# First products of eight channel blocks ahead of the norm: a hybrid attention block on one Trainium2 core

## The chip, the core and the metric

One core of a Trainium2 chip runs the whole kernel: TensorE (PE; its weight load is the row PEld), VectorE (DVE), ScalarE (ACT), GpSimd (POOL) and SyncE (SP), which issues most of the transfers. SBUF has 128 partitions, and TensorE adds up in PSUM. The metric is the device time of one execution in microseconds (us). The three runs shown of the kernel before have a median of 1760.35 us (1759.39 to 1760.63).

## The reference, cut to what matters

A layer works on 256 latent tokens `x` and 256 context tokens `ctx`, each of 2048 channels. The change touches its first step only, the modulated RMS norm and the input projection:

```python
sh1, sc1, g1, sh2, sc2, g2 = jnp.split(jax.nn.silu(c) @ w_ada[l] + b_ada[l], 6, axis=-1)
csh1, csc1, ... = jnp.split(jax.nn.silu(c_ctx) @ w_ada[l] + b_ada[l], 6, axis=-1)
... = split_columns(modulate(rmsnorm(x, norm_mix[l]), sh1, sc1) @ w_in[l])
... = split_columns(modulate(rmsnorm(ctx, norm_mix[l]), csh1, csc1) @ w_in[l])
# rmsnorm(x, w) = x * rsqrt(mean(x * x) + eps) * w;  modulate(x, shift, scale) = x * (1 + scale) + shift
```

So the input of the projection is h = x · a · r + shift, where a = w(1 + scale) and the shift go by channel and the norm r by token. Everything else (latent attention, a gated DeltaNet in both directions, the merge, a gated MLP) comes behind it and is the same in both kernels.

## The kernel before, in words

Channels lie on partitions: 16 blocks of 128 channels (`KD`), and 2 × 256 tokens as columns (latent and context, the two streams s). All products are done with a high and a low half: a number is rounded to the type fp32r (its high half), and the rest is its low half; a product is high·high + high·low + low·high. `load_w` and `split` make the halves of a weight, ScalarE the high (line 123), VectorE the low (line 124), in six buffers each.

The first stage runs in an order written out by hand. `pe`, `oact`, `odve` and `osync` are engines whose instructions keep the order of the program (`Ordered`); instructions of the plain `act`, `dve`, `sync` are placed by the compiler's scheduler between them. It goes as follows:

- The scale and the shift by channel come from products of `silu(c)` with 4096 columns of `w_ada`, in two ways. `mod_mm` (16 products of 256 columns, 32 output rows each, tile `amp`) and `mod_cols` (turn the row into columns, tiles `aas` for a and `shs` for the shift) give two blocks at once from a quad of 512 KB weight tiles. `scale_dot` gives the scale of one block on VectorE, by two dots of 2048 elements (tile `junk`) with rows that `spread` copied to all partitions (tile `scb`). The blocks in `SCP`, counted in pairs, get their scale in the first way, the others by dots; every shift comes in the first way.
- Squares of x and ctx (tile `sq`), their sum over channels (`square_sum`, tile `pss`), the norm r on GpSimd and its broadcast to a tile `bc` come ahead of the first product.
- Then block by block (loop over k at line 481): `first_hi` casts the weight of 864 columns (96 + 6 × 128) to its high half `gh`; `h_prep` takes x · a · r, adds the shift and makes both halves of h (two fused multiplies, two activations, two fused adds, and the weight's low half `gl`); `first_mm` does 7 column tiles × 2 streams × 3 products, added up over all 16 blocks in 7 PSUM banks (`fp`). Between the tiles lie the modulation products of later blocks, behind them the dots.
- The seven sums are copied to `krd` and `dkx`, and the general projections (`proj`, tile `mmp`) go on with all 16 blocks of h, which stays in SBUF (`H`).

SP issues the loads in written order; a load waits for its buffer, and so do the loads behind it. There are 8 tiles of 512 KB (`raw`: quads of `mod_mm`, later the weights of `proj` and of the modulation's rest), 4 of 1 MB (`wt`) and 3 of a first weight's 432 KB (`gr`).

Of the kernel before, what the change touches and what calls it, by code (L numbers as in the profile page):

```python
# [45 lines left out]
NW = 4  # L46
SCP = (0, 2, 4, 6)
# [8 lines left out]
def hybrid_block(ctx: ExitStack, tc: tile.TileContext, io, dbg=None):  # L56
# [285 lines left out]
    def mod_cols(p, scale, amp, row):  # L342
# [3 lines left out]
        for j in range(2):  # L346
            k = slice(2 * p + j, 2 * p + j + 1)
            out, mul, add = (aas, nmix[:, k], b1[:, k]) if scale else (shs, 1.0, bada[:, k])
            oact.activation(out[:, 2 * p + j], amp[:, T + 2 * j : T + 2 * j + 2], AF.Identity, bias=add, scale=mul)

    def load_scale(k):
        w = pa2.tile([P, D], F32, tag="wt", name="wt", bufs=NW)
        osync.dma_start(w, io["wadas"][k])
        return w

    scm = {}
# [10 lines left out]
    def load_first(k):
        gr = pa2.tile([P, G3], F32, tag="gr", name="gr", bufs=3)
        osync.dma_start(gr, io["wfirst"][k])
        return gr  # L370

    def first_hi(k):

        g = [pa2.tile([P, G3], F32R, tag=n, name=n) for n in ("gh", "gl")]
        oact.copy(g[0], grs[k])
        return g

    def h_prep(k, gh, gl):

        late = k and k % 2 == 0 and k // 2 in SCP  # L380
        if late:
            odve.tensor_tensor(out=gl, in0=grs.pop(k), in1=gh, op=ALU.subtract)
        for s, xs in enumerate((xl, xc)):
            odve.scalar_tensor_tensor(out=xs[:, k], in0=xs[:, k], scalar=aas[:, k, s : s + 1], in1=(bc if k else bcp)[:, s], op0=ALU.mult, op1=ALU.mult)
        if not late:
            odve.tensor_tensor(out=gl, in0=grs.pop(k), in1=gh, op=ALU.subtract)
        for s, xs in enumerate((xl, xc)):
            oact.activation(H[s][:, k, 0], xs[:, k], AF.Identity, bias=shs[:, k, s : s + 1], scale=1.0)
        for s, xs in enumerate((xl, xc)):
# [1312 lines left out]
```

## Time and profile before

| | us |
|---|---|
| median of the runs shown | 1760.35 |
| the profiled execution | 1757.95 |
| its span, first to last instruction | 1756.1 |
| TensorE busy in the span | 1733.0 |
| VectorE busy | 1333.7 |
| ScalarE busy | 943.1 |
| first product of the first stage starts at | 29.1 |
| first product of the projections starts at | 141.06 |

The profile is of one execution. Its rows give the start or the number of instructions, busy time, engine, line and operation, and in brackets the idle time of the engine just before with what ended it. Nearly all instructions of the ordered engines carry line 70, that of the helper which records them, so they are told apart by their tiles. The engines wait for each other through semaphores, and idle time of an engine costs only where TensorE, busy 99% of the span, ends up waiting for it.

### The profile page before, as it was taken

The numbers are of one execution on the slowest core, as the hardware profiler recorded it, in microseconds if no ns is written. First come the engines' busy times: TensorE is split into PE (matmuls) and PEld (weight loads), VectorE is DVE, ScalarE is ACT, GpSimd is POOL, SyncE is SP. The second block draws the span as 40 slices with busy tenths as digits, with TensorE's granted clock in tenths as the row PEclk, the third lists the DMA queues.
The fourth block names the chain that finished last, engine by engine and source line by source line (L and its number), as shares of the span: only waits on it lengthen the run. The fifth ranks groups of instructions, "written<-read, shape, count | busy, mean of one in ns | idle before, by whom it ended". The sixth has DMA issues, their size and how long they took to land.

```text
span 1756.1 us, 34353 instructions
## 1 busy us (share of the span) xinstructions
PE 1733.0 (99%) x13093; PEld 1507.0 (86%) x13093; DVE 1333.7 (76%) x2608; ACT 943.1 (54%) x1953; POOL 48.5 (3%) x49
## 2 busy tenths in 40 slices
PE   8999999999999999999999999999999999999999
PEld 6787888888888888888888888888888888888888
DVE  4688887679888778686789788887787888655554
ACT  4235545454566756665665555555555555544443
POOL 0000001000000000000000000000000000000000
PEclk9999999999999999999999999999999999999999
DMA  9993788683788777897958757777667777566662
GB/s 383 392 374 130 204 257 239 204 275 108 242 248 244 237 240 245 289 331 262 340 167 264 266 176 254 237 231 234 188 217 223 228 227 226 177 203 202 193 198 89
DMA packets 188566, 414.56 MB, mean 236 GB/s; under 512 B 56752, under 2 KB 95024, under 8 KB 186096
## 3 DMA queue, kind: packets, MB, share of 16 engines
q1 hardware_dynamic: 162800, 397.39, 69.9%
q10 hardware_dynamic: 25600, 14.96, 2.8%
q8 instruction: 103, 1.69, 0.4%
q14 instruction: 63, 0.52, 0.1%
HBM read 385.69 MB, written 26.48 MB: 235 GB/s over the span
## 4 chain that ended last, share of the span: by engine, by line
PE 89%; DMA 5%; DVE 3%; issue 1%; ACT 1%; SPq 0%; POOL 0%; POOLq 0%; ACTq 0%; DVEq 0%
PE fps L70 27%; PE dps L70 14%; PE mmp L70 13%; PE gtp L70 10%; PE brp L70 5%; PE ops L70 4%; PE fp L70 4%; DMA raw<-in_wadab 1%; PE vps L70 1%; PE amp L70 1%; PE kps L70 1%; DVE wlo L124 1%; PE tp L70 1%; DMA rawa<-in_wada 1%; PE kp L70 1%
## 5 line engine op out<-in xcount | busy, mean ns | idle before, releaser
L124 DVE TENSOR_TENSOR wlo<-raw,whi 128x512 fp32r<-128x512 f32 (+1 forms) x940 | 635.4, 685 | 211.0 <-ACT whi L123 200.0
L123 ACT CAST whi<-raw 128x512 fp32r<-128x512 f32 (+1 forms) x940 | 574.4, 619 | 377.7 <-PE dps L70 113.7
L70 PE MATMUL fps<-H,whi 128*128 128x512 f32 x1376 | 472.6, 392 | 1.4 <-DVE H L1537 1.4
L70 PE MATMUL fps<-H,wlo 128*128 128x256 f32 x1376 | 371.5, 280 | 0.0
L70 PEld LDWEIGHTS fps<-H,whi 128*128 128x128 f32 x1376 | 252.5, 188 | 52.6 <-ACT whi L123 1.7
L70 PEld LDWEIGHTS fps<-H,wlo 128*128 128x128 f32 x1376 | 258.5, 188 | 7.6 <-DVE wlo L124 0.7
L70 PE MATMUL gtp<-h,whi 128*128 128x512 f32 x640 | 230.4, 397 | 1.0 <-ACT whi L123 1.0
L70 PE MATMUL mmp<-h,whi 128*128 128x512 f32 x640 | 227.2, 397 | 0.1
L70 PE MATMUL dps<-GB,whi 128*128 128x512 f32 (+1 forms) x595 | 195.7, 378 | 0.0
L70 PE MATMUL mmp<-h,wlo 128*128 128x256 f32 x640 | 175.4, 281 | 0.0
L70 PE MATMUL gtp<-h,wlo 128*128 128x256 f32 x640 | 172.8, 280 | 0.5 <-DVE wlo L124 0.5
L70 PE MATMUL dps<-GB,wlo 128*128 128x256 f32 x560 | 154.1, 280 | 0.0
L70 PEld LDWEIGHTS gtp<-h,whi 128*128 128x128 f32 x640 | 119.5, 188 | 26.3 <-ACT whi L123 1.5
L70 PEld LDWEIGHTS mmp<-h,whi 128*128 128x128 f32 x640 | 119.0, 188 | 25.4 <-DVE kvx L515 0.7
L70 PEld LDWEIGHTS dps<-GB,whi 128*128 128x128 f32 x595 | 109.2, 188 | 21.1
L70 PEld LDWEIGHTS gtp<-h,wlo 128*128 128x128 f32 x640 | 120.5, 188 | 5.1 <-DVE wlo L124 0.8
L70 PEld LDWEIGHTS mmp<-h,wlo 128*128 128x128 f32 x640 | 120.3, 188 | 2.4 <-issue 0.2
L70 PEld LDWEIGHTS dps<-GB,wlo 128*128 128x128 f32 x560 | 105.1, 188 | 0.6
L274 DVE CUSTOM_DVE_ANT_0 rawa<-rawa,sch 128x1024 f32<-128x1024 f32 x64 | 78.1, 1222 | 32.4 <-DMA rawa<-in_wada 32.3
L70 PE MATMUL fp<-h,gh 128*128 128x256 f32 (+1 forms) x448 | 83.9, 288 | 0.9 <-DVE h L70 0.9
L70 DVE CUSTOM_DVE_ANT_0 rawa<-rawa,sch 128x1024 f32<-128x1024 f32 x64 | 77.7, 1217 | 0.0
L70 PEld LDWEIGHTS fp<-h,gh 128*128 128x128 f32 (+1 forms) x448 | 68.4, 187 | 6.4 <-issue 4.5
(568 smaller groups left out, 2543.0 us busy)
## 6 DMA issues: line engine op xcount, KB each, us to landing
rawa<-in_wada SPq DMA_DIRECT2D x128, 512.0 KB, 4.8
raw<-in_wgate SPq DMA_DIRECT2D x82, 512.0 KB, 4.6
raw<-in_wval SPq DMA_DIRECT2D x82, 512.0 KB, 4.9
raw<-in_wdown SPq DMA_DIRECT2D x80, 512.0 KB, 4.1
wt<-in_wadas SPq DMA_DIRECT2D x16, 1024.0 KB, 10.1
raw<-in_wadab SPq DMA_DIRECT2D x32, 512.0 KB, 11.6
raw<-in_wgm SPq DMA_DIRECT2D x32, 512.0 KB, 4.7
raw<-in_wgd SPq DMA_DIRECT2D x32, 512.0 KB, 6.0
```

The costliest lines, as they stand in the source:

```text
L70: i = f(*a, **k)
L123: act.copy(hi, raw)
L124: dve.tensor_tensor(out=lo, in0=raw, in1=hi, op=ALU.subtract)
L274: (odve if ada.bound else dve).tensor_tensor_reduce(out=w, in0=w, in1=sch, scale=1.0, scalar=0.0, op0=ALU.mult, op1=ALU.add, accum_out=par ...
```

## The change

For channel blocks 0 to 7 (`K0` = 8) the products start from x · a alone (`h_early`): neither the norm nor the shift is needed. After block 7 each of the seven sums is multiplied by the norm and moved from PSUM to its place in `krd` or `dkx` (`half_way`); the bank then starts anew with block 8. Blocks 8 to 15 are done as before, with norm and shift in h. At the end the second half is added to the first. The shift of blocks 0 to 7 is a constant by output column and stream: `shift_mm` multiplies the shift with the unsplit first weights of these blocks, which are loaded a second time for it (kinds "r" and "q" of `load`), `shift_cols` turns the row into columns, and an activation adds them as its bias.

The later projections need h of all blocks with norm and shift. So blocks 0 to 7 are prepared a second time (letter R: two fused multiplies, two activations, two fused adds), R0 to R2 beside blocks 13 to 15, R3 to R7 between the final additions; the first projection (weights `wdk` of head 3) runs over blocks 8 to 15 first (`turned`).

The squares are taken on ScalarE in four parts beside the products and added on VectorE (`add_squares`), so that TensorE sums one part instead of four; their sum stands between column tiles of block 6. Pairs 0, 1, 3 and 5 get their scale from `mod_mm`, each as a quad of `raw` tiles; blocks 4, 5, 8, 9 and 12 to 15 by dots. Shifts of pairs 4 to 7 are computed at blocks 7 to 12, those of pairs 0 to 3 at blocks 13 to 15. The 20 warming products ahead of the first product are gone, and there are 3 tiles of 1 MB instead of 4. h is kept as two tiles of 8 blocks for each stream (`Halves`).

The order is now text, read by `run`: L load (W, s: a quad for scale or shift; w: a row for dots; g: a first weight; x: parts of x and ctx), G cast of a weight, E early block, F products (block, from tile, to tile), W and S modulation products, C their columns, D dots, Q squares, A addition of squares, V `half_way`, N scaling and the weight's low half, H shift and halves, R both again. `token_scale` and `token_bcast` are the norm and its broadcast, with the instructions of before.

```diff
-NW = 4
-SCP = (0, 2, 4, 6)
+NW = 3
+SCP = (0, 1, 3, 5)
+K0 = 8
...
+    dst = [krd.rearrange("p a b -> p (a b)")] + [dkx[:, j].rearrange("p a b -> p (a b)") for j in range(2 * N1)]
...
+        elif kind == "r":
+            t = pa2.tile([P, D], F32, tag="wt", name="wt", bufs=NW)
+            for i in range(2):
+                rts[2 * n + i] = t[:, i * GR : i * GR + G3]
+                osync.dma_start(rts[2 * n + i], io["wfirst"][2 * n + i])
...
+    def h_early(k):
+
+        for s, xs in enumerate(x2):
+            oact.activation(H[s][:, k, 0], xs[:, k], AF.Copy, scale=aas[:, k, s : s + 1])
+        first_lo(k)
+        for s, xs in enumerate(x2):
+            odve.scalar_tensor_tensor(out=H[s][:, k, 1], in0=xs[:, k], scalar=aas[:, k, s : s + 1], in1=H[s][:, k, 0], op0=ALU.mult, op1=ALU.subtract)
+
+    def h_scale(k):
+        for s, xs in enumerate(x2):
+            odve.scalar_tensor_tensor(out=xs[:, k], in0=xs[:, k], scalar=aas[:, k, s : s + 1], in1=bc[:, s], op0=ALU.mult, op1=ALU.mult)
+
+    def h_shift(k):
+        for s, xs in enumerate(x2):
+            oact.activation(H[s][:, k, 0], xs[:, k], AF.Identity, bias=sh(k)[:, s : s + 1], scale=1.0)
+        for s, xs in enumerate(x2):
+            odve.scalar_tensor_tensor(out=H[s][:, k, 1], in0=xs[:, k], scalar=sh(k)[:, s : s + 1], in1=H[s][:, k, 0], op0=ALU.add, op1=ALU.subtract)
+
...
+    def square(q):
+        for s, xs in enumerate(x2):
+            oact.activation(Sq[q][s], xs[:, 4 * q : 4 * q + 4], AF.Square)
+
+    def add_squares(q):
+        for s in range(2):
+            odve.tensor_tensor(out=Sq[0][s], in0=Sq[0][s], in1=Sq[q][s], op=ALU.add)
+
+    def square_sum():
+        pss = psa.tile([P, 512], F32, tag="aux", name="pss")
+        for s in range(2):
+            for j in range(4):
+                pe.matmul(pss[32 * j : 32 * j + 32, s * T : s * T + T], ones.broadcast_to([P, 32]), Sq[0][s][:, j], start=s == 0, stop=s == 1)
+        oact.copy(bcf, pss)
+
...
+    def half_way(j):
+        m = FW[j][1]
+        odve.tensor_tensor(out=dst[j], in0=first_ps[j][:m], in1=bcf[:m], op=ALU.mult)
+
+    def shift_mm(crow, a, b):
+
+        o, e = FW[a][0], FW[b - 1][0] + P
+        ps = psa.tile([P, 512], F32, tag="aux", name="shp")
+        for k in range(K0):
+            j = slice(32 * (k % 4), 32 * (k % 4) + 32)
+            pe.matmul(ps[j, : e - o], csh[:, k], rts[k][:, o:e], start=k < 4, stop=k >= 4)
+        oact.copy(crow[:, o:e], ps[:, : e - o])
+
+    def shift_cols(crow):
+        ps = psa.tile([P, 2 * N1 + 1, 2], F32, tag="aux", name="shc")
+        for n, (o, m) in enumerate(FW):
+            for j in range(m // 32):
+                pe.matmul(ps[32 * j : 32 * j + 32, n], crow[:, o + 32 * j : o + 32 * j + 32], sel[:, :2], start=True, stop=True)
+        oact.copy(ccol[:96], ps[:96])
+        oact.copy(ccol[96:, 1:], ps[96:, 1:])
+
...
+            elif c == "N":
+                h_scale(*n)
+                first_lo(*n)
+            elif c == "H":
+                h_shift(*n)
+            elif c == "R":
+                h_scale(*n)
+                h_shift(*n)
...
+    run("LW0 Lg0 Lx0 Lg1 LW1 Lx1 Lg2")
+    for s in range(2):
+        for q in range(4):
+            spread(s, q)
+    run("G0 W0 C E0 Lw4 Lg3 Lw5 Lx2")
+    run("""
+        G1 F0,0,7 E1 Lg4 LW3
+        G2 F1,0,3 W1 F1,3,5 C E2 F1,5,7 Q0 Lg5 Lx3
+        G3 F2,0,7 E3 D4 Lg6 Lx4 Lw8 Ls4
+        G4 F3,0,7 E4 D5 Q1 A1 Lg7 Lw9
+        G5 F4,0,7 E5 Lg8
+        G6 F5,0,2 W3 F5,2,4 C E6 F5,4,7 Q2 A2 Q3 A3 Lg9 Ls5
+        G7 F6,0,2 E7 F6,2,4
+    """)
+    square_sum()
+    for t in H:
+        t.more()
+    run("F6,4,6")
+    ms = token_scale()
+    run("F6,6,7 D8 Lg10 G8 F7,0,1")
+    token_bcast(ms)
+    run("""
+        F7,1,3 S4 F7,3,5 C F7,5,7 V0 V1 V2 N8 V3 H8 V4 V5 V6 LW5
+        G9 D9 F8,0,2 S5 F8,2,4 C F8,4,7 N9 H9 Lg11 Lw12 Ls6 Lw13
+        G10 W5 F9,0,2 C N10 H10 F9,2,7 D12 Lg12 Ls7 Lw14
+        G11 F10,0,2 S6 F10,2,4 C F10,4,7 N11 H11 D13 Lg13 Lw15 Ls0
+        G12 F11,0,7 N12 H12 D14 Lg14 Lr0 Lr1
+        G13 F12,0,2 S7 F12,2,4 C F12,4,7 N13 H13 Lg15 Ls1 D15 Lr2
+        G14 F13,0,2 S0 F13,2,4 C F13,4,7 N14 H14 Ls2 Lq6 R0
+    """)
+    tc.keep_in_program_order(act.dma_start(Sc.rearrange("h p i -> p h i"), scb[:, 0].rearrange("p (h i) -> p h i", h=2)))
+    run("""
+        G15 F14,0,2 S1 F14,2,3 C F14,3,5 N15 H15 Ls3 Lq7 S2 F14,5,6 C F14,6,7 R1 R2
+        F15,0,1 S3 F15,1,2 C F15,2,4
+    """)
+    crow = wr.tile([P, GR], F32, tag="raw", name="crow", bufs=NR)
+    shift_mm(crow, 0, 4)
+    first_mm(15, 4, 5)
+    shift_mm(crow, 4, 2 * N1 + 1)
+    first_mm(15, 5, 2 * N1 + 1)
+    shift_cols(crow)
+    for j, (o, m) in enumerate(FW):
+        odve.tensor_tensor(out=dst[j], in0=first_ps[j][:m], in1=dst[j], op=ALU.add)
+        t = krd if j == 0 else dkx[:, j - 1]
+        for s in range(2):
+            act.activation(t[:, s], t[:, s], AF.Identity, bias=ccol[:m, j, s : s + 1], scale=1.0)
+        if j in (1, 2, 4, 5, 6):
+            run(f"R{3 + (1, 2, 4, 5, 6).index(j)}")
...
+        for i in range(KD):
+            k = (i + K0) % KD if turned else i
```

More of the change, by code (lines that the diff above doesn't have):

```diff
@@ L346, in mod_cols @@
         for j in range(2):
[L347 to L356, printed above, removed]
+            n = 2 * p + j
+            k = slice(n, n + 1)
+            out, mul, add = (aas[:, n], nmix[:, k], b1[:, k]) if scale else (sh(n), 1.0, bada[:, k])
+            oact.activation(out, amp[:, T + 2 * j : T + 2 * j + 2], AF.Identity, bias=add, scale=mul)
     def scale_dot(k, s):
@@ L364, in scale_dot @@
         if s:
+            wts.pop(k)
             odve.tensor_scalar(out=aas[:, k], in0=scm.pop(k), scalar1=nmix[:, k : k + 1], scalar2=b1[:, k : k + 1], op0=ALU.mult, op1=ALU.add)
[L367 to L370, printed above, removed]
     def first_hi(k):
[L374 to L389, printed above, removed]
-            odve.scalar_tensor_tensor(out=H[s][:, k, 1], in0=xs[:, k], scalar=shs[:, k, s : s + 1], in1=H[s][:, k, 0], op0=ALU.add, op1=ALU.subtract)
@@ L419, in hybrid_block @@
-    Sq = ph.tile([P, KD, 2, T], F32, tag="h", name="sq")
-    def square(s, e, a, b):
-        x = (xl, xc)[s][:, a:b]
-        if e is oact:
-            e.activation(Sq[:, a:b, s], x, AF.Square)
-        else:
-            e.tensor_tensor(out=Sq[:, a:b, s], in0=x, in1=x, op=ALU.mult)
-    def square_sum(q):
-        for j in range(4):
-            pe.matmul(pss[32 * j : 32 * j + 32], ones.broadcast_to([P, 32]), Sq[:, 4 * q + j].rearrange("p a b -> p (a b)"), start=q == 0, stop=q == 3)
-    def scale_mm(p):
-        return mod_mm([wts[2 * p + m // 2][:, m % 2 * GR : m % 2 * GR + GR] for m in range(4)])
@@ L451, in hybrid_block @@
-    msp = psa.tile([P, 4], F32, tag="aux", name="msp")
-    for n in range(4):
-        col_sum(msp[:, n : n + 1], bcf[:, n * P : n * P + P], sel[:, 2:3])
-    ms = pa2.tile([P, 4], F32, tag="ms", name="ms", bufs=1)
-    odve.tensor_scalar(out=ms, in0=msp, scalar1=1.0 / D, scalar2=EPS, op0=ALU.mult, op1=ALU.add)
-    rsq(pa2, ms, ms, 4)
-    spread(1, 3)
-    bc_ps = psa.tile([P, 512], F32, tag="aux", name="bc_ps")
-    for n in range(4):
-        pe.matmul(bc_ps[:, n * P : n * P + P], ms[:, n : n + 1].broadcast_to([P, P]), ident, start=True, stop=True)
@@ L508, in hybrid_block @@
-    pe.pinned = False
-    for s in range(2):
-        dump(f"h{s}", H[s].bitcast(F32))
+                pe.matmul(ps, lo, H[s][:, k, 0], start=False, stop=k % K0 == K0 - 1 and s == 1)
+        if b > 2 * N1:
+            hks.pop(k)
+    def square(q):
[4 more added lines that the diff above has]
+            odve.tensor_tensor(out=Sq[0][s], in0=Sq[0][s], in1=Sq[q][s], op=ALU.add)
@@ new lines, in square_sum, with token_scale @@
+    def square_sum():
[4 more added lines that the diff above has]
+        oact.copy(bcf, pss)
+    def token_scale():
+        msp = psa.tile([P, 4], F32, tag="aux", name="msp")
+        for n in range(4):
+            col_sum(msp[:, n : n + 1], bcf[:, n * P : n * P + P], sel[:, 2:3])
+        ms = pa2.tile([P, 4], F32, tag="ms", name="ms", bufs=1)
+        odve.tensor_scalar(out=ms, in0=msp, scalar1=1.0 / D, scalar2=EPS, op0=ALU.mult, op1=ALU.add)
+        rsq(pa2, ms, ms, 4)
+        return ms
@@ L1549, in hybrid_block @@
     pe.pinned = False
-    dump("h2", H2.bitcast(F32))
     pM.close()
```

213 lines of the change are left out of this document (104 added, 109 removed).

## The prediction

> **What bounds the kernel now.** I read the page's summary and chain first, then busy time by stage, then the chain and the timeline of the first stage, which is where the change lies.
>
> ```profile
> span 1756.1 us, 34353 instructions
> PE 1733.0 (99%) x13093; PEld 1507.0 (86%) x13093; DVE 1333.7 (76%) x2608; ACT 943.1 (54%) x1953; POOL 48.5 (3%) x49
> PE 89%; DMA 5%; DVE 3%; issue 1%; ACT 1%; SPq 0%; POOL 0%; POOLq 0%; ACTq 0%; DVEq 0%
> ```
> TensorE bounds the kernel. The windows (columns: sum, PE, PEld, DVE, ACT, POOL busy, granted clock, DMA share, GB/s) show where it does not:
>
> ```profile
> 0.00:29.00 29.00, 22.69 (x252) 16.06 (x252) 9.92 (x23) 11.90 (x21) 2.29 (x10) 1.00 0.95 367
> 29.00:60.00 31.00, 27.24 (x264) 20.44 (x264) 20.09 (x29) 8.92 (x20) 0.00 (x0) 0.89 1.02 418
> 60.00:141.00 81.00, 81.00 (x892) 72.39 (x891) 63.64 (x97) 31.16 (x65) 0.00 (x0) 1.00 0.90 352
> 141.00:200.00 59.00, 58.82 (x349) 46.94 (x349) 49.96 (x105) 30.48 (x62) 1.93 (x1) 1.00 0.51 162
> ```
> Up to 60 us the 16 DMA engines are full and the first products run at a mean clock of 0.89; from 60 us TensorE has no gap. The first product starts at 29.1 us, the stage ends near 141.1 (124.07 + 17.15, less the overlap with the next product). The chain of waits prices TensorE's pieces, and the timeline the start and the one slow place:
>
> ```profile
> 53.20 2.80 PE fp L70 x12
> 84.35 1.86 PE amp L70 x32
> 86.21 1.58 PE fp L70 x12
> 87.79 0.24 PE amp L70 x16
> 96.86 8.68 PE fp L70 x72
> 124.07 17.15 PE fp L70 x144
> ```
> ```profile
> 4.31 5.58 PE L70 MATMUL scp<-ident,sc 128*128 128x128 f32 x32 [4.31 <-DVE sc L305]
> 11.06 1.16 PE L70 MATMUL scp<-ident,sc 128*128 128x128 f32 x8
> 21.36 1.93 PE L70 MATMUL amp<-wt,csf 128*32 128x256 f32 x32
> 24.16 0.60 ACT L70 ACTIVATE aas<-amp,b,vecs 128x2 f32<-128x2 f32 x2 [0.43 <-PE amp L70]
> 30.18 0.36 PE L70 MATMUL fp<-h,gh 128*96 128x256 f32 x1 [0.72 <-DVE h L70]
> 25.61 0.64 PE L70 MATMUL amp<-raw,csf 128*32 128x256 f32 x8 [0.15 <-DMA raw<-in_wadab]
> 48.53 0.69 PE L70 MATMUL amp<-raw,csf 128*32 128x256 f32 x8 [2.01 <-DMA raw<-in_wadab]
> ```
> A product costs 17.15/144 = 0.119 us, a channel block (42 products) 5.02; a modulation product with its column step 1.86 + 0.24 + the restart, 3.68 - 12 x 0.119 = 2.25 us.
>
> **The start moves forward.** The squares, their sum, the norm and the shift of block 0 no longer stand ahead of the first product. What stays: eight spreads (four end at 9.9, four more at 1.1 each: 14.3), W0 (1.93: 16.2). From the end of W0's product to a scale column the present run takes 24.5 - 23.3 = 1.2 us, then 0.5 for ScalarE's high half and 0.5 for VectorE's low half. W0's weights are there: now the last of pair 0's shift lands at 25.5 us after 8.6 MB, at 418 GB/s that is 5.1 us + MB/0.42, and W0's 2.1 MB behind the 0.2 of the vectors land at 10.6. So steady products begin at 18.7 instead of 30.0, **11.3 us earlier**.
>
> **What TensorE has to do from there.** 16 x 5.02 = 80.3. Modulation products: twelve before and after, but eleven instead of ten now come behind the first product: 24.8. Squares' sum 0.9 (eight products of 256 columns where a modulation product has sixteen at 1.86), column sums twice a column step, 0.5, broadcast as a spread 1.1: 2.5. The shift's own products have 8 x (480 + 384) columns against 16 x 256 of a modulation product, 1.69 x 1.86 = 3.1, and 27 small column products at 0.24/8 are 0.8. Sum 111.5: 18.7 + 111.5 = **130.2 without a wait**. The same sum for the kernel before gives 30.0 + 80.3 + 22.5 = 132.8 against 141.1; of the 8.3 missing 4.9 are the wait for the shift of pair 2 (46.5, by the clock's windows below, to 53.2, less its 1.86) and 1.4 the twelve products behind it, 2.80 for 1.43. About 2 stay unexplained, in the first 60 us; from there to 141 the sum fits.
>
> **The waits that come in.** VectorE and ScalarE run in written order. Their prices, by start to start:
>
> ```profile
> 62.22 0.49 ACT L70 ACTIVATE h<-xc,shs 128x256 fp32r<-128x256 f32 x1
> 64.47 0.92 ACT L70 CAST gh<-gr 128x864 fp32r<-128x864 f32 x1 [1.75 <-PE fp L70]
> 65.36 0.48 DVE L70 SCALAR_TENSOR_TENSOR xl<-xl,aas,bc 128x256 f32<-128x256 f32 x1
> 65.76 0.48 DVE L70 SCALAR_TENSOR_TENSOR xc<-xc,aas,bc 128x256 f32<-128x256 f32 x1
> 66.15 1.05 DVE L70 TENSOR_TENSOR gl<-gr,gh 128x864 fp32r<-128x864 f32 x1
> 67.12 0.48 DVE L70 SCALAR_TENSOR_TENSOR h<-xl,shs,h 128x256 fp32r<-128x256 f32 x1
> 67.91 2.29 DVE L70 CUSTOM_DVE_ANT_0 junk<-wt,scb 128x2048 bf16<-128x2048 f32 x1
> 70.25 0.29 DVE L70 TENSOR_SCALAR aas<-scm,vecs,b 128x2 f32<-128x2 f32 x1
> 70.44 2.28 DVE L70 CUSTOM_DVE_ANT_0 junk<-wt,scb 128x2048 bf16<-128x2048 f32 x1
> ```
> ```profile
> 8.70 1.22 DVE L70 TENSOR_TENSOR sq<-xc 128x1024 f32<-128x1024 f32 x1
> 9.83 1.28 DVE L70 COPY scb<-scp 128x512 f32<-128x512 f32 x2
> 15.06 1.06 ACT L70 ACTIVATE sq<-xl 128x1024 f32<-128x1024 f32 x1
> ```
> A fused multiply is 0.40, the weight's low half 0.97, so an early block (E) 1.77 and a full one (N and H) 2.57; a scale row's two dots (D) 2.34 + 2.34 + 0.19 = 4.87; an addition of squares (A) 2 x 1.15 = 2.3; a square of four blocks and both streams on ScalarE (Q) 2 x 1.0. VectorE's work grows: A1 to A3 take 6.9 where it squared for 4.4 ahead of the first product, seven scalings (V) come in, and R0 to R2.
>
> V (a PSUM tile times a row tile) is not in the trace; the nearest rows are
>
> ```profile
> 141.26 1.89 DVE L528 COPY dkx<-fp 128x512 f32<-128x512 f32 x3 [1.60 <-PE fp L70]
> 174.78 0.76 DVE L515 TENSOR_TENSOR cx<-mmp,cx 128x256 f32<-128x256 f32 x2
> ```
> a copy from PSUM at 0.63 and two half-wide additions from PSUM at 0.38 each: between 0.63 and 0.76; I take 0.65, by the equal shape, 4.6 for seven.
>
> *Block 5.* F0 ends at 23.7, F1 with W1 at 31.0. Behind E2 ScalarE squares (Q0) until 33.0, and the weight of block 3 is cast only then, until 33.9. VectorE follows: E3 to 35.7, D4 to 40.5, E4 to 42.3, D5 to 47.2, A1 to 49.5, E5's first low half usable at 51.0. TensorE: F2 31.2 to 36.2, F3 to 41.2, 0.7 of wait for E4, F4 to 47.0, and then F5 stands behind D5 and A1: **4.0**, in which it does one product of 0.1. *Sum of squares.* Behind W3's columns ScalarE owes columns 0.6, E6 0.8, Q2 and Q3 4.1, then VectorE half of A3 twice 1.2 + 0.3, together 7.2; TensorE has F5,4 to F6,3 meanwhile, seven tiles of 0.72: 5.0. It waits **2.2**. *Blocks 8 to 15.* With V at 0.65 block 8 waits 0.6. Where a block has no modulation product between, VectorE's 4.87 + 2.57 = 7.4 stands against 5.0 of TensorE: block 12 (F11 has none) waits 1.6; blocks 9, 13 and 14 have one and stay under 0.3 each, 0.5 together. *End of the loads.* Eight weights are loaded a second time, 3.5 MB, 8.4 us at 0.42 MB/us, in an order where each quad of shift weights needs the quad before last consumed; DMA has some 10% free from 60 us on. Laid out behind each other the last of S2's weights lands 0.3 and S3's 1.6 us late: **1.9**; the cover gone altogether it would be 5, the transfer of one quad. Sum of waits 0.7 + 4.0 + 2.2 + 0.6 + 1.6 + 0.5 + 1.9 = 11.5: 130.2 + 11.5 = 141.7.
>
> **The clock.** What a hole does is in the present trace:
>
> ```profile
> 46.00:48.00 2.00, 0.52 (x5) 0.32 (x3) 1.97 (x3) 0.00 (x0) 0.00 (x0) 1.00 1.02 416
> 48.00:50.00 2.00, 1.03 (x12) 0.38 (x16) 1.93 (x6) 0.62 (x2) 0.00 (x0) 0.75 1.06 438
> 50.00:52.00 2.00, 1.81 (x16) 0.20 (x8) 1.44 (x3) 0.29 (x1) 0.00 (x0) 0.50 0.99 415
> 52.00:54.00 2.00, 1.88 (x12) 1.07 (x13) 0.00 (x0) 0.37 (x1) 0.00 (x0) 0.50 1.03 429
> 54.00:56.00 2.00, 2.00 (x16) 1.83 (x19) 0.00 (x0) 0.00 (x0) 0.00 (x0) 0.55 1.00 416
> ```
> Two empty us (46.5 to 48.5), then sparse ones, and the clock is at half from 49 to 55.8; products resume at 53.2, so 1.4 is lost on the twelve of the chain's row. A hole of 4.0 is longer, so I count one loss of 1.4 to 2.0, 1.7, at block 5; the 2.2 at the sum of squares is just the length that was enough here, spread otherwise: 0.6 (0 to 1.7). At the start the 20 warming products are gone and some 1.6 us of 2.5 behind W0 are empty; the first 29 us of now, 22.7 of them busy, show 1.00 throughout, so 0 (up to 1.7). Stage end 141.7 + 2.3 = **144.0, 2.9 later than before**.
>
> The Trainium skill, "TensorE: Matmul & The Clock Gate", section "What's actually happening", has the clock fall to half after at least one idle window of about 3.4 us, in windows that run free of the kernel. The trace has it fall after 2.2 empty us and some sparse ones; by the page's rule the hole at the sum of squares would cost nothing and that at block 5 perhaps nothing, and the time would be 1762 to 1763.
>
> **Behind the stage.** Blocks R3 to R7 (4 x 0.40 each, 8.0) and seven additions (4.6) replace three copies (1.9): 10.7 more on VectorE, about 6 of it beside F15. The first projection starts with blocks 8 to 15 for two streams, 8 x 0.71 = 5.7 us, so R7 has time. The gate preparation moves back by 3 to 4 us on a VectorE that had 59 - 50 = 9 us free until 200, and no wait of TensorE longer than this one was to be seen from 141 to 260:
>
> ```profile
> PE cps L70 <- issue: 0.2, 1, 0.2
> ```
> Bounds: -1 (the additions free PSUM sooner than the copies) to 5 (half the backlog passed on); I take 1, nearer the cover.
>
> **Sum.** The profiled execution took 1757.95, 1.85 around its span. +2.9 + 1 = 3.9 gives 1761.9 by its measure; the median of the runs shown stands 2.4 higher (0.14%), so **1764.2**.
>
> **Rivals.** *The products do not wait* (faster): VectorE has 8 x (1.77 + 4.87 + 2.57) + 6.9 + 4.6 + 4.8 = 90 us of work for 112 of TensorE, so if its order holds up TensorE only at E4, block 8 and S3 (4 us) and no clock is lost, the stage ends at 134.2, 6.9 earlier: 1753.5 to 1755. For it: the total; against it: the two holes follow from written order with 4.0 and 2.2 to spare, block 5's decided once D5 and A1 together pass 3 us. *The backlog is passed on* (slower still): if VectorE's later gate and E tiles hold back the weight splits once its 9 free us are used, 4 us more, and the start runs cold (1.7): 1770. For it: VectorE's 85% from 141 to 200; against: no wait there now. *Gain and loss cancel*: the hole at block 5 costs no clock and nothing is passed on: 3.3 less, 1761.
>
> **Chances.** Forecast 0.48 (its own range 1760 to 1769), the products do not wait 0.22, the backlog 0.18, cancelling 0.12. A change under 0.2% (3.5 us) cannot be told from none by a measurement of this kernel: above 1763.9 lie some 0.3 of the forecast's 0.48 and the backlog, in all 0.48; faster is the first rival with little beside, 0.23; same 0.29. The range takes in the first rival's lower half and the backlog: 1752.5 to 1770.5.
>
> **What would show it.** Right: first product at 18 to 19 us; a TensorE wait of 3 to 4 us for VectorE ahead of block 5, with D5 and A1 just before on VectorE; one near 2 us at the sum of squares; granted clock under 0.8 near 50 us; first mmp product at 142 to 146. Wrong: block 5 without a wait, or a stage end before 138, or new TensorE waits between 145 and 220.

## The result, and the profile after

The changed kernel takes **1788.34 us** (median of 6 runs, 1787.28 to 1789.99) against 1759.49 of the kernel before beside it (6 runs, 1756.93 to 1760.63): ratio 1.0167, interval 1.0154 to 1.0180. That is 28.9 us slower, where 4 were forecast, and outside the range. All medians in this document are of fast executions: of the last kernel one execution, of 7440.65 us at a mean granted clock of 0.216, is not counted. Span and busy engines of the profiled execution, from the page:

```profile
span 1786.1 us, 34564 instructions
PE 1744.1 (98%) x13143; PEld 1513.3 (85%) x13143; DVE 1348.5 (75%) x2637; ACT 956.1 (54%) x1986; POOL 50.6 (3%) x50
```

To see where the time went, cut both executions at the first product of the projections (`mmp`) and at the first head's column sums (`sp`). Columns are those of the windows in the prediction: sum, PE, PEld, DVE, ACT and POOL busy, granted clock, DMA share, GB/s. First the kernel before, then the changed one:

```profile
0.00:141.06 141.06, 130.99 (x1404) 108.95 (x1405) 93.65 (x148) 51.98 (x104) 2.29 (x10) 0.98 0.94 369
141.06:194.95 53.89, 53.71 (x286) 42.26 (x285) 47.41 (x101) 28.78 (x59) 0.00 (x0) 1.00 0.49 159
194.95:1756.10 1561.15, 1548.32 (x11406) 1355.79 (x11405) 1192.61 (x2360) 862.39 (x1790) 46.16 (x39) 1.00 0.72 227
```
```profile
0.00:155.06 155.06, 135.52 (x1454) 111.09 (x1455) 97.82 (x151) 54.17 (x110) 4.51 (x11) 0.94 0.87 338
155.06:221.73 66.67, 58.45 (x292) 45.24 (x284) 59.03 (x127) 39.38 (x86) 0.00 (x0) 0.92 0.53 179
221.73:1786.10 1564.37, 1550.15 (x11406) 1356.93 (x11405) 1191.61 (x2360) 862.51 (x1791) 46.13 (x39) 1.00 0.71 226
```

The first stage ends 14.0 us later (2.9 were forecast). The 54 us behind it, which I call the stretch, grow by 12.8 (1 was forecast). In the stretch TensorE is empty for 8.2 us instead of 0.2 (66.67 - 58.45 and 53.89 - 53.71), and busy for 4.7 us longer with six products more, at a mean clock of 0.92. The rest, with the same 11406 matmuls, differs by 3.2.

**The first stage.** Its start and its holes, from the timeline (start, duration, engine, line, operation; in brackets the idle time before and what ended it):

```profile
17.48 0.36 PE L71 MATMUL fp<-h0a,gh 128*96 128x256 f32 x1 [1.11 <-ACT h0a L71]
...
47.94 2.35 DVE L71 TENSOR_TENSOR sq<-sq 128x1024 f32<-128x1024 f32 x2
48.63 0.36 PE L71 MATMUL fp<-h0a,gh 128*96 128x256 f32 x1 [0.71 <-ACT h0a L71]
51.72 0.36 PE L71 MATMUL fp<-h0a,gh 128*96 128x256 f32 x1 [2.73 <-DVE h0a L71]
...
64.70 0.64 PE L71 MATMUL pss<-sq,ones 128*32 128x256 f32 x8 [0.96 <-DVE sq L71]
65.75 0.64 PE L71 MATMUL pss<-sq,ones 128*32 128x256 f32 x8 [0.41 <-DVE sq L71]
68.51 2.28 DVE L71 CUSTOM_DVE_ANT_0 junk<-wt,scb 128x2048 bf16<-128x2048 f32 x1
68.68 2.99 POOL L180 TENSOR_TENSOR ms<-ms,half 128x4 f32<-128x4 f32 x1 [66.60 <-DVE ms L71]
70.83 2.29 DVE L71 CUSTOM_DVE_ANT_0 junk<-wt,scb 128x2048 bf16<-128x2048 f32 x1
71.72 1.16 PE L71 MATMUL bc_ps<-ident,ms 128*128 128x128 f32 x8 [1.76 <-POOL ms L180]
```

The start, the hole at block 5 and the one at the sum of squares are where the prediction put them. The last four rows it did not have: GpSimd's power for the norm takes 2.99 us instead of 1.02, while row 8's two dots run on VectorE, and TensorE waits 1.76 for it. The granted clock, last but two in each row, falls at the start and behind block 5:

```profile
16.00:20.00 4.00, 2.66 (x29) 2.34 (x30) 2.45 (x5) 3.02 (x8) 0.00 (x0) 0.86 1.04 413
20.00:24.00 4.00, 4.00 (x27) 4.00 (x26) 0.51 (x2) 0.00 (x0) 0.00 (x0) 0.71 1.04 430
...
52.00:56.00 4.00, 4.00 (x39) 2.36 (x41) 1.03 (x2) 0.00 (x0) 0.00 (x0) 0.63 0.92 328
...
136.00:140.00 4.00, 3.62 (x26) 1.76 (x22) 0.00 (x0) 0.37 (x1) 0.00 (x0) 0.50 1.01 406
140.00:144.00 4.00, 4.00 (x37) 3.29 (x40) 2.31 (x6) 2.12 (x6) 0.00 (x0) 0.50 1.02 416
```

The half clock of the last two rows follows a wait for the weights of S2, the third late shift product. The timeline of the two queues and of TensorE there, and then the waits of SP's queue (total, times, longest):

```profile
121.69 10.82 SPq L71 DMA_DIRECT2D raw<-in_wadab  x4
124.45 0.39 ACTq L577 DMA_DIRECT2D Sc<-scb  x1
129.46 0.64 PE L71 MATMUL amp<-raw,csf 128*32 128x256 f32 x8
135.01 1.08 PE L71 MATMUL amp<-raw,csf 128*32 128x256 f32 x8 [4.91 <-DMA raw<-in_wadab]
```
```profile
SPq L71 <- DMA Sc<-scb: 9.1, 1, 9.1
```

SP needs 10.8 us to issue the four loads of S2 (2.2 for the next four, from 133.07 us on), because one of them waits 9.1 us for ScalarE's store of `Sc`, 1 MB, which has nothing to do with its data.

**Behind the stage.** TensorE has next to no wait in the kernel before; now it has these two, and a lower clock behind each (0.50 from 168 to 172 us, 0.67 from 204 to 208):

```profile
PE mmp L71 <- DVE wlo L125: 3.6, 1, 3.6
PE mmp L71 <- DVE cx L600: 2.6, 1, 2.6
```

VectorE is behind in both. How far shows in the chain of small operations on the gate columns (copies `g`, then `gd` to `ghl`, from which the decay tiles E are made), which starts later and takes longer. Kernel before, then changed kernel:

```profile
142.84 0.40 ACT L555 COPY g<-krd 32x256 f32<-32x256 f32 x1
145.21 0.59 DVE L561 COPY gd<-gps 64x128 f32<-64x128 f32 x2 [1.93 <-PE gps L70]
156.04 0.23 DVE L124 TENSOR_TENSOR ghl<-gx,ghl 128x64 fp32r<-128x64 f32 x1 [0.31 <-ACT ghl L123]
```
```profile
158.64 0.40 ACT L629 COPY g<-krd 32x256 f32<-32x256 f32 x1
161.01 0.59 DVE L635 COPY gd<-gps 64x128 f32<-64x128 f32 x2 [0.49 <-PE gps L71]
182.70 0.24 DVE L125 TENSOR_TENSOR ghl<-gx,ghl 128x64 fp32r<-128x64 f32 x1
```

From the first `mmp` product to `ghl` are 27.6 us instead of 15.0. The experiments ask which of the new work does that, and what each piece of the first stage costs.

### The profile page after: what moved, and what is told of

Same layout as the page of the kernel before. It is cut to its first block, busy times and chain, and to the rows that moved or that the text cites. A ratio compares the mean times of both kernels' runs of the same rounds, so it can differ in the third digit from the quotient of the medians.

```text
span 1786.1 us, 34564 instructions
## 1 busy us (share of the span) xinstructions
PE 1744.1 (98%) x13143; PEld 1513.3 (85%) x13143; DVE 1348.5 (75%) x2637; ACT 956.1 (54%) x1986; POOL 50.6 (3%) x50
## 4 chain that ended last, share of the span: by engine, by line
PE 83%; DMA 2%; DVE 2%; issue 1%; ACT 0%; POOL 0%; SPq 0%; ACTq 0%; DVEq 0%; POOLq 0%
PE fps L71 26%; PE dps L71 13%; PE gtp L71 12%; PE mmp L71 11%; PE brp L71 5%; PE ops L71 3%; PE vps L71 1%; PE kps L71 1%; DMA rawa<-in_wada 1%; PE sps L71 1%; PE tp L71 1%; PE qps L71 1%; PE kp L71 1%; PE ivp L71 1%; DVE wlo L125 1%; PE op L71 1%
## 5 line engine op out<-in xcount | busy, mean ns | idle before, releaser
L71 PE MATMUL fps<-H2b,whi 128*128 128x512 f32 x688 | 246.3, 392 | 1.4 <-DVE H2b L1612 1.4
L71 PE MATMUL fps<-H2a,whi 128*128 128x512 f32 x688 | 243.1, 393 | 0.1
L71 PE MATMUL fps<-H2a,wlo 128*128 128x256 f32 x688 | 192.6, 280 | 0.1
L71 PE MATMUL fps<-H2b,wlo 128*128 128x256 f32 x688 | 178.9, 280 | 0.0
L71 PEld LDWEIGHTS fps<-H2b,whi 128*128 128x128 f32 x688 | 129.1, 188 | 26.6 <-ACT whi L124 1.7
L71 PEld LDWEIGHTS fps<-H2a,whi 128*128 128x128 f32 x688 | 129.1, 188 | 26.0 <-DVE H2a L1612 0.3
L71 PEld LDWEIGHTS fps<-H2a,wlo 128*128 128x128 f32 x688 | 129.3, 188 | 4.0 <-DVE wlo L125 0.5
L71 PEld LDWEIGHTS fps<-H2b,wlo 128*128 128x128 f32 x688 | 129.1, 188 | 3.7 <-DVE wlo L125 0.2
L71 PE MATMUL gtp<-h0b,whi 128*128 128x512 f32 x320 | 117.1, 397 | 0.0
L71 PE MATMUL gtp<-h0a,whi 128*128 128x512 f32 x320 | 115.7, 398 | 1.0 <-ACT whi L124 1.0
```

The lines of the kernel that those rows point to most:

```text
L71: i = f(*a, **k)
```

## The experiments

Each is an edit of the changed kernel. "Start" is the first `mmp` product, "stretch" the time from there to `sp`; the changed kernel has 155.1 and 66.7, the kernel before 141.1 and 53.9. In the expectations theories A to E are named where they come up.

**The store of Sc issued early**

```diff
     run("F6,4,6")
+    tc.keep_in_program_order(act.dma_start(Sc..., scb[:, 0]...))
...
-    tc.keep_in_program_order(act.dma_start(Sc..., scb[:, 0]...))     # was behind block 14
```

> The store of the scale rows (Sc, 1 MB, issued by ScalarE behind block R0) moves forward to the products of block 6; nothing else changes. Theory A: the loads of S2's weights stand 9 to 11 us behind that store, because the issues take eight DMA semaphores in turn and one of S2's loads has the semaphore of the store. Then the wait of 4.9 us ahead of S2 and the spread of its four pieces go (7 us), the half clock behind them too (3 us): the first projection starts at 144 to 147 us instead of 155.1 and the time falls by 8 to 11 us. Theory B (the prediction's: buffers and bandwidth of the second load of the first weights set S2's landing): within 2 us of the changed kernel.

Measured 1782.47 us, ratio 1.0122 (1.0107 to 1.0138): 5.9 us less than the changed kernel by the medians. Start 148.6, stretch 67.7. The store leaves at 65.8 us, and the 4.9 us wait is gone; what is left, in TensorE's waits from 110 to 148 us:

```profile
PE amp L71 <- DMA raw<-in_wadab: 3.0, 6, 0.6
```

Theory A has the mechanism, since the wait is gone; its size missed, 5.9 us against 8 to 11, and the start came 1.6 us later than its bound of 147. The listing of the program's waits says what ties the load to the store: in this program the DMAs that SP and ScalarE issue take eight semaphores in turn, and these two have the same.

```
SP  80 L71  DMA raw<-in_wadab 128x1024 [waits DMAHW5_49,PE_49]
ACT 90 L577 DMA Sc<-scb 128x2x1024 [waits DMAHW5_49]
```

**The end of the stage in another order**: additions 0 to 3 and R3 to R5 ahead of the shift's own products, R6 ahead of its columns, R7 behind the first of the shift's additions. Then both this and the early store.

```diff
+    add_half(0); add_half(1); run("R3"); add_half(2); run("R4"); add_half(3); run("R5")
     shift_mm(crow, 0, 4)
     first_mm(15, 4, 5)
+    add_half(4)
     shift_mm(crow, 4, 2 * N1 + 1)
     first_mm(15, 5, 2 * N1 + 1)
+    run("R6"); add_half(5); add_half(6)
     shift_cols(crow)
```

> Only the order at the end of the first stage changes: the additions 0 to 3 and blocks R3 to R5 are written ahead of the shift's products, R6 between, R7 behind the first bias. Theory A: VectorE's backlog behind the stage comes from order, since ScalarE's activations of R3 stand behind the shift columns' copies, so that VectorE idles some 9 us around 149 to 158 and has everything to do at once later. Then the waits of TensorE behind the stage (3.6 for a weight's low half, 2.6 for an addition) and two stretches of half clock go: 7 to 12 us less, and from the start of the first projection to the first head's column sums 55 to 60 us instead of 66.7 (54.0 before). Theory B: VectorE's 10.7 us of more work do not fit whatever the order: 0 to 3 us less.

> The store forward and the new order of the tail together. If both causes are separate the gains add: 15 to 22 us less than the changed kernel, 1766 to 1773, which leaves the waits of the first half of the stage (block 5, sum of squares, norm) with their half clock, some 5 to 8 us over the kernel before. If S2's wait only hid the backlog, clearly less than the sum.

Measured 1792.05 (ratio 1.0177, 1.0162 to 1.0193) and, with the early store, 1784.07 (1.0135, 1.0118 to 1.0152): 3.7 us more than the changed kernel and 4.3 less, so both expectations missed. In the first the stretch fell by 2.7 us only, to 64.0, and the start came 4.5 us later: the copy of the shift's row stood behind R3 to R5 in ScalarE's order, and TensorE waited 3.1 us for it. This order is not the cure.

**R3 to R7 left out**: the later projections use the h of blocks 3 to 7 without norm and shift.

```diff
-        if j in (1, 2, 4, 5, 6):
-            run(f"R{3 + (1, 2, 4, 5, 6).index(j)}")
```

> Blocks R3 to R7 are left out (the later projections take h of blocks 3 to 7 without norm and shift); the additions stay. Theory A and B both: the work that makes the backlog is gone, 8 to 13 us less, and the stretch from the first projection to the head's column sums near 54 to 57 us. Theory C (the backlog comes from the weight splits, six of which were done ahead of the first projection before and one or two now, since the loads come late): less than 4 us less.

Measured 1786.07 (2 runs, 1784.9 to 1787.23; ratio 1.0143, 1.0123 to 1.0163): the stretch fell from 66.7 to 63.6 only. By the bounds written down that is theory C, but the view of ScalarE shows that it is no clean test of R. With nothing between them, the twelve additions of the shift to the other columns now stand ahead of the gate copies:

```profile
157.39 4.89 ACT L593 ACTIVATE dkx<-dkx,ccol 128x256 f32<-128x256 f32 x12
162.30 0.40 ACT L627 COPY g<-krd 32x256 f32<-32x256 f32 x1
```

So either something else makes the stretch long (theory C: weights loaded and split too late), or the shift that is added ahead of the gate columns does (theory D).

**The shift part left out; then its loads too**

```diff
-    crow = ...; shift_mm(crow, 0, 4); ...; shift_cols(crow)
+    first_mm(15, 4, 2 * N1 + 1)
     for j, (o, m) in enumerate(FW):
         odve.tensor_tensor(out=dst[j], in0=first_ps[j][:m], in1=dst[j], op=ALU.add)
-        act.activation(t[:, s], t[:, s], AF.Identity, bias=ccol[...], scale=1.0)
-        run("R...")                                # R0 to R2 as well
...
-    Ls0 Lr0 Lr1 Ls1 Lr2 Ls2 Lq6 Ls3 Lq7 S0 S1 S2 S3    # second kernel only
```

> Left out: the shift's own products, their row and columns, the shift added to the sums, and R0 to R7 (so the later projections use the scaled, unnormed h of blocks 0 to 7). The four late shift quads are still loaded and multiplied with the modulation. Stretch means first mmp product to the first head's column sums: 53.9 us in the kernel before, 66.7 in the changed one, 63.6 without R3 to R7. Theory C, the raw ring held by the late shift quads keeps the next weights from being loaded and split ahead: the stretch stays at 61 to 64 us, time 1780 to 1784. Theory D, what stands at the stage's end in written order (shift products, row copies, columns, the shift added ahead of the gate columns) makes the gate chain late: the stretch falls to 54 to 57 us, and the time is 1770 to 1775.

> As the kernel without the shift part, and the four late shift quads and the eight second loads of first weights are left out too, with their modulation products. Theory C (the ring held by the late quads): only now the stretch falls, to 54 to 57 us, with weight splits ahead of the first mmp product again (6 in the kernel before, 1 to 2 in the changed one). Theory D: the stretch is 54 to 57 us here as in the kernel with only the shift part left out. By both the first mmp product comes at 131 to 136 us and the time is 1750 to 1757, without the half clock at 136 to 147 us.

Measured 1770.87 (ratio 1.0062, 1.0045 to 1.0079) and 1754.49 (0.9972, 0.9962 to 0.9982). The stretch is **52.0** with the late quads still loaded and multiplied, 53.2 without: by the bounds theory D, and C falls, since neither kernel has a split on VectorE ahead of its first `mmp` product. Both leave out R0 to R7 too, so they do not tell the shift's part from R's; the kernels with the rewritten end, below, compute both. The gate chain, in the first of the two, starts with the projections and takes 10.0 us:

```profile
153.15 0.58 DVE L625 COPY gd<-gps 64x128 f32<-64x128 f32 x2
163.16 0.22 DVE L125 TENSOR_TENSOR ghl<-gx,ghl 128x64 fp32r<-128x64 f32 x1
```

The late quads and the second loads matter ahead of it: without them the start is 134.2 instead of 152.9. (The kernel before multiplies those four quads too, so 1754.49 is no gain over it.)

**The early blocks in another order**

```diff
-  G1 F0,0,7 E1 Lg4 LW3
+  G1 F0,0,7 E1 D4 Lg4 LW3
-  G2 ... E2 F1,5,7 Q0 Lg5 Lx3 / G3 F2,0,7 E3 D4 ...
+  G2 ... E2 F1,5,7 Lg5 Lx3 / G3 F2,0,7 E3 Q0 D5 ...
-  G4 F3,0,7 E4 D5 Q1 A1 ... / G5 F4,0,7 E5 Lg8
+  G4 F3,0,7 E4 Q1 A1 ... / G5 F4,0,7 E5 Q2 A2 D8 Lg8
-  G6 ... F5,4,7 Q2 A2 Q3 A3 ... / F6,6,7 D8 Lg10 ...
+  G6 ... F5,4,7 Q3 A3 ... / F6,6,7 Lg10 ...
```

> Only the written order of the early blocks changes: scale row 4's dots right behind block 1, block 0 to 3's squares behind block 3, the addition of squares a block later, the second squares and addition behind block 5, row 8's dots ahead of the sum of squares instead of beside GpSimd's pow. Theory A, the first-stage waits of this page are lost time (3.1 us ahead of block 5 with a half clock behind it, 1.4 us at the sum of squares, 2.0 us of a longer pow, 1.8 us of TensorE behind it): the first mmp product comes 6 to 9 us earlier, at 146 to 149, and the time is 1779 to 1783. Theory B, the loads set the pace of the stage, so TensorE only reaches the next wait for a transfer sooner: the first mmp product comes 0 to 2 us earlier, new waits for raw or wt tiles between 70 and 135 us, and the time is 1786 to 1789.

Measured 1779.23 (ratio 1.0109, 1.0092 to 1.0125): 9.1 us less than the changed kernel, start 146.2, so theory A. The waits at block 5 and at the sum of squares are gone, and the power is short again without a dot beside it:

```profile
60.95 1.02 POOL L180 TENSOR_TENSOR ms<-ms,half 128x4 f32<-128x4 f32 x1 [58.88 <-DVE ms L71]
```

**Early store and early order together, without and with 11 warming products ahead of the first product**

```diff
-    run("G0 W0 C E0 Lw4 Lg3 Lw5 Lx2")
+    run("G0 W0"); warm(3); run("C"); warm(8)       # second kernel only
+    run("E0 Lw4 Lg3 Lw5 Lx2")
```

> The early order and the early Sc store, without the 11 warming products. If the granted clock at the start (0.86 at 16 to 20 us, 0.71 at 20 to 24 us in the changed kernel) costs what its windows say, 1.2 to 1.8 us, this takes 1.2 to 1.8 us more than with the warming products (1773.1), 1774 to 1775. If the loads set the pace behind it, the difference is 0 to 0.3 us.

> Nothing left out. The early order, the Sc store issued some 60 us earlier, and 11 warming products ahead of the first product (3 behind the first scale product, 8 behind its columns). If the three add up (6 to 9, 5.9 and about 1 us) the first mmp product comes at 139 to 143 and the time is 1772 to 1776. If the loads set the pace instead, the early order gives nothing here: first mmp product at 147, time 1781 to 1783. By both the stretch behind stays at 64 to 68 us.

Measured 1772.26 (ratio 1.0064, 1.0044 to 1.0084) without and 1773.11 (1.0069, 1.0051 to 1.0087) with them. The two mends add up: 5.9 + 9.1 = 15.0, measured 15.2 to 16.1. The warming products do what they should to the clock, first without, then with them:

```profile
20.00:24.00 4.00, 4.00 (x25) 4.00 (x25) 0.75 (x2) 0.00 (x0) 0.00 (x0) 0.66 1.03 428
```
```profile
20.00:24.00 4.00, 4.00 (x36) 4.00 (x36) 0.62 (x2) 0.69 (x1) 0.00 (x0) 1.00 1.03 429
```

and the start moved from 140.0 to 137.7 in these executions, but no gain is to be seen in the times, whose intervals overlap. The expected 1.2 to 1.8 us are not shown.

**The end of the stage rewritten for the gate columns**, with the three mends, and alone:

```diff
-  S2 F14,5,6 C F14,6,7 R1 R2 / F15,0,1 S3 F15,1,2 C F15,2,4
+  S2,14,4 R1 R2 R3 U4 U5 F15,0,1 C B0 T4 T5 U6 U7 F15,1,2    # S2,14,4: a tile of block 14 behind each piece
+  S3,15,2 B1 B2 B3 F15,5,6 C T6 T7 B4 B5                     # U, T: the two halves of R; B: the addition
   shift_mm(crow, 0, 4)
+  run("F15,6,7 B6"); shift_cols(crow, 0, 4); add_shift(0)    # gate block first
   shift_mm(crow, 4, 2 * N1 + 1)
+  # gate copies; then shift_cols(crow, 4, 7); add_shift(j) only where a head takes dkx
-  ccol = pa3.tile(...); sel = pa3.tile(...)
+  ccol = mid.tile(...); sel = mid.tile(...)
```

> Nothing left out: the three mends together, and the stage's end rewritten so that the gate columns do not stand behind the shift: products of blocks 14 and 15 between the pieces of S2 and S3, R1 to R7 and the additions ahead of the shift's own products, the shift columns of the gate block first and the others behind the gate copies, the shift of the other columns added only where a head needs them. Theory D (what stands at the stage's end makes the gate chain late): the stretch from the first mmp product to the first head's column sums falls from 66 to 54 to 58 us, the first mmp product comes at 134 to 137 us, and the time is 1755 to 1763. If the added work on VectorE and ScalarE itself makes the stretch long, wherever it stands, the stretch stays at 62 to 66 and the time is 1765 to 1770.

> Only the stage's end rewritten as in the kernel with the gate columns first; the early order, the Sc store and the start are as in the changed kernel. Theory D: the stretch falls from 66.7 to 54 to 59 us and the first mmp product comes 0 to 4 us earlier, time 1774 to 1781. If the added work itself makes the stretch long: stretch 62 to 66, time 1783 to 1788.

Measured 1779.22 (ratio 1.0104, 1.0081 to 1.0126) and 1793.27 (1.0187, 1.0165 to 1.0210). The stretch did fall, to **54.6** and **53.9**, with all of R0 to R7 and the shift computed: theory D, against the rival that the added work makes it long wherever it stands. (R3 to R7 stand ahead of the projections now, and the shift of the other columns with the heads that use them; which of these moves counts for how much was not told apart.) But the times missed by 16 and 12 us. In both, TensorE's products of S3 waited 3.5 us for a ScalarE that stood behind R1 to R3, which is part of why the start came only at 147.2 and 162.2:

```profile
PE amp L71 <- ACT csh L71: 3.5, 1, 3.5
```

And 1.2% were lost far behind: from 1100 to 1500 us TensorE did 2277 products where the changed kernel did 2306. What differs there is where tiles lie, the split weights among them: two small tiles in the pool ahead of them had moved them from a multiple of 64 bytes to 32 past one.

**Mended, and the addresses alone.** The first kernel has R1 to R3 ahead of S2, the gate copies with their shift on VectorE, and `sel` padded to 64 bytes; the second is the changed kernel with a 32-byte tile and nothing else.

```diff
+  Ls3 Lq7 R1 R2 R3 U4 U5 S2,14,4 F15,0,1 C ...
+  sel = mid.tile([P, 16], F32, name="sel")[:, :3]
+  odve.tensor_scalar(out=g2[...], in0=krd[64:96], scalar1=ccol[64:96, 0, s], op0=ALU.add)
...
+  pool.memset(mid.tile([P, 8], F32, name="pad"), 0.0)        # second kernel only
```

> As the kernel with the gate columns first, with R1 to R3 ahead of S2 in ScalarE's order (there S3's first piece waited 3.5 us for a ScalarE standing behind them), the gate copies with their shift on VectorE, and the split weights on addresses that are a multiple of 64 bytes again (there a small tile had moved them to 32 past one). Theory D: first mmp product at 140 to 144 us, stretch 53 to 56, time 1756 to 1762. Theory E (the addresses of the split weights made the last 650 us of that kernel slower, 571 products of TensorE in 100 us where all others do 577 to 579): from 1100 us on 577 to 579 products in 100 us again. If the loss behind the stage comes from the new order itself, 571 to 572 as there and a time of 1770 to 1776.

> The changed kernel with nothing but a 32-byte tile ahead of the split weights, so that they lie 32 bytes past a multiple of 64. Theory E: 571 to 572 products of TensorE in each 100 us from 1100 us on instead of 578 to 579, and a time 8 to 16 us longer than the changed kernel's 1788.3: 1796 to 1804. If addresses don't matter: 578 to 579, and 1787 to 1790.

Measured **1762.46** (ratio 1.0013, 1.0004 to 1.0022) and 1800.74 (1.0242, 1.0219 to 1.0265). Theory E holds: 32 bytes alone cost 12.4 us by the medians (12.0 of them behind `sp`, in the profiled executions). The windows from 1100 to 1500 us of the changed kernel, of that kernel and of the mended one:

```profile
1100.00:1500.00 400.00, 400.00 (x2306) 351.61 (x2305) 323.36 (x629) 221.60 (x434) 0.00 (x0) 1.00 0.71 226
```
```profile
1100.00:1500.00 400.00, 399.96 (x2278) 349.78 (x2278) 320.27 (x622) 219.07 (x428) 0.00 (x0) 1.00 0.69 223
```
```profile
1100.00:1500.00 400.00, 400.00 (x2301) 352.66 (x2300) 321.90 (x624) 222.19 (x434) 0.00 (x0) 1.00 0.70 221
```

Theory D reaches the end now: start 139.8, stretch 55.7, 10.7 us less than with the three mends alone. The gate chain is ahead of the projections and takes 8.7 us:

```profile
139.09 0.59 DVE L651 COPY gd<-gps 64x128 f32<-64x128 f32 x2 [1.26 <-PE gps L71]
147.82 0.23 DVE L125 TENSOR_TENSOR ghl<-gx,ghl 128x64 fp32r<-128x64 f32 x1 [0.31 <-ACT ghl L124]
```

**The last 2.8 us.** One kernel closes small gaps ahead of the start (one addition and a head's shift are moved too); the other puts the two small tiles into another pool, so that the split weights lie where they lie in the kernel before (in the mended one they lie 128 bytes on).

```diff
-  shift_mm(crow, 0, 4); run("F15,6,7 B6"); shift_cols(crow, 0, 4); shift_mm(crow, 4, 7)
+  shift_mm(crow, 0, 4); shift_mm(crow, 4, 7); shift_cols(crow, 0, 4); run("F15,6,7 B6")   # first kernel
-  ccol = mid.tile(...); sel = mid.tile([P, 16], ...)[:, :3]
+  ccol = px.tile(...); sel = px.tile([P, 3], ...)                                         # second kernel
```

> As the kernel with the gate columns first and the weights aligned, with both of the shift's own products side by side and the last product tile behind the first shift columns, to close the gaps of 0.3 to 0.7 us ahead of the first mmp product (2.3 empty us from 130 to 140 us, and a granted clock of 0.70 from 140 to 150 behind them). If those gaps cause the half clock: clock above 0.9 from 140 to 150, and 1757 to 1760. If not: 1761 to 1763.

> The kernel with the gate columns first and aligned weights, with its two small tiles moved to another pool, so that the split weights lie at the addresses of the kernel before (there they lay 128 bytes on, and TensorE did 2301 products from 1100 to 1500 us, where the kernel before and the changed one do 2306). If the addresses make the last loss: 2305 to 2306 products, the part behind the first head's column sums 1561 to 1564 us instead of 1566, and a time of 1757.5 to 1760.5. If they don't: 2301 products and 1761 to 1764.

Measured 1761.75 (ratio 1.0017, 1.0007 to 1.0028) and 1761.06 (1.0012, 1.0001 to 1.0024). The gaps were not closed: new ones took their place (1.4 us for the gate copies), and the clock was 0.50 from 140 to 144 us as in the mended kernel, so that run tells nothing on its question. The addresses did bring the rate back, 2305 products, and the part behind `sp` to 1563.6 us; but the median did not follow: it is 0.6 us above the bound of 1760.5. The profiled execution of this kernel took 1759.37 us, and its granted clock did not fall, where the mended kernel's did. First the mended one, then this:

```profile
130.00:140.00 10.00, 7.73 (x134) 4.21 (x133) 7.65 (x20) 7.17 (x22) 0.00 (x0) 0.96 0.43 156
140.00:144.00 4.00, 4.00 (x12) 3.05 (x13) 4.00 (x14) 4.00 (x11) 0.00 (x0) 0.50 1.03 402
```
```profile
130.00:140.00 10.00, 8.10 (x136) 4.58 (x136) 7.55 (x19) 6.60 (x20) 0.00 (x0) 1.00 0.40 142
140.00:144.00 4.00, 3.30 (x17) 2.61 (x18) 3.93 (x15) 4.00 (x11) 0.00 (x0) 1.00 1.03 393
```

Of its executions the four with a mean granted clock of 0.998 or more have a median of 1758.4 us, the seven below it 1763.0; the kernel before beside it has 1758.6 and 1760.8. So the last 2 to 3 us go with the clock of the single execution. What in the kernel makes it fall more often stays open. No version that computes everything beat the kernel before.

## Why the prediction was wrong

The side was right (slower, at 0.48), the size was not: 28.9 us instead of 4. Step by step:

- **The start moves forward**: right. The first product is at 17.5 and the steady ones begin at 18.0, 12.2 us ahead of before; 18.7 and 11.3 were forecast (the terms written there, 16.2 + 1.2 + 0.5 + 0.5, give 18.4).
- **Block 5**: right, by its cause too. 0.7 us for E5's high half and 2.7 for its low half behind D5 and A1, together 3.4 for a forecast of 4.0; behind it the clock falls to 0.63 for 4 us, 1.5 us lost for a forecast of 1.7. The Trainium skill, "TensorE: Matmul & The Clock Gate", section "What's actually happening", by which a hole of this length might cost nothing, disagrees with this row, and the time of 1762 to 1763 that hung on it falls (with the terms of the sum it would have been 1762 to 1763.6).
- **Sum of squares**: right place, 1.4 us instead of 2.2 (the terms written there give 7.0 and so 2.0), and the clock stays at 1.00 from 60 to 100 us, where 0.6 was counted. **V**: three of them take 1.88, so 0.63; 0.65 was taken. **Blocks 8 to 15**: 1.3 us in one block instead of 2.7 in several.
- **The power on GpSimd** had no term. In the kernel before it took 1.02 us, with no dot beside it; I left it so. The change puts row 8's dots right behind the sum of squares, beside it: 2.99, and 1.8 us of TensorE. The early order, without that neighbour, has 1.02. The Trainium skill, "SBUF — State Buffer", section "SBUF: two separate sides", has GpSimd and a VectorE operation with two inputs from SBUF lock each other out for a whole instruction; the rows agree in part. The power ends 0.9 us after the first dot, as if it had waited for it; but the second dot starts at 70.83, before the power's end at 71.67, and takes its usual 2.29.
- **The clock at the start** was set at 0, with 1.7 as its bound. It fell to 0.86 and 0.71, 0.6 + 1.2 = 1.8 us by the windows, though warming it up showed no gain in the time.
- **End of the loads**: the first step that failed. I counted 1.9 us, from the ring of tiles and from the rate of the DMA engines, and not what else an issue waits for. The store of `Sc` stands behind block 14 in ScalarE's order in both kernels (it leaves at 127.98 us in the one before), but there SP had no loads for this stage left to issue. The change put those of S2 and S3 behind it: a wait of 4.9 us, the half clock after it, 5.9 us in the time.
- **Behind the stage**: the step that failed most, 12.8 us for a forecast of 1 and a bound of 5. "About 6 us of it beside F15" and "R7 has time" were sums of VectorE's work, and as sums they were not wrong: with the order rewritten the same work is covered (stretch 53.9 to 55.7). What I did not follow is the chain of dependencies. The gate columns `krd` now wait for the last shift product, its row, its column and an addition, and so their first copy comes 3.6 us behind the first projection instead of 1.8; the gate chain is then interleaved with R3 to R7 and with weight splits that VectorE did ahead of the projections before, and takes 21.7 us instead of 10.8. The E tiles land on the next head's work, and TensorE waits twice, 6.2 us in all, with a lower clock behind each wait.

The rival "the backlog is passed on" had the mechanism, in part, and 4 us for it. The parts that the runs priced, by the medians: the early order (block 5, sum of squares, power, their clocks) 9.1, the store 5.9, the end of the stage 10.7; together 25.7 of 28.9. The rest was not told apart from the clock of single executions.

A small slip of the working: 42 products at 0.119 are 5.00 us and not 5.02, 0.3 us over 16 blocks.

"The products do not wait" (1753.5 to 1755) was the other side. It priced a stage that ends 6.9 us earlier than before. Computed in full, none here started the projections more than 3.4 us earlier (the three mends, 137.7): of the waits for VectorE and ScalarE 0.8 and 0.5 us are left there, but the last shift weights then come up to 0.6 us late each, 2.6 us in all.

## What to carry to other kernels

When a change moves work to the end of a stage, follow the first small result that the next stage needs through every queue that it now stands behind; a sum of busy time beside a cover says nothing of it. For each load that becomes urgent, ask what large transfers are under way when it is issued, on other queues too: it may have to wait for one of them to land. And an operation's duration holds for the neighbours that it had.

## What the runs showed of the hardware

- **Addresses of matmul operands.** With the split weights 32 bytes past a multiple of 64, TensorE did 2278 products in 400 us instead of 2306, 1.2% fewer, at a granted clock of 1.00: 12.4 us on the whole kernel, from one 32-byte tile. At 128 bytes on (a multiple of 64 still) it did 2301. The split weights are the operand that TensorE loads. The rows of these loads have a median of 188 ns in both kernels, and those of the products of 512 columns (`fps`, second half of the blocks) 396 instead of 392, with ends that are modelled; so which of the two pays, the load of the weights or the product, stays open.
- **The clock** fell to 0.50 from 140 to 144 us although no gap ahead of it was longer than 0.74 us (mended kernel, 2.3 empty us spread over 130 to 140 us), and in an execution of the last kernel with 1.9 empty us there it did not.
- **A load can wait for a store that it shares nothing with**: 9.1 us, by a semaphore that this program gives to both of them in turn.
